# First attention layer of a two-layer diffusion trunk: both halves of a unit's value product in one attention step

## The chip, the cores and the metric

The kernel runs on one core of one Trainium2 chip. Times are device microseconds (us) of a whole execution. An execution's profile gives its span from the first to the last instruction; what lies around the span is the rest of the execution's time.

## The reference

The network has two layers over 1024 latent tokens and 256 context tokens, 1024 channels, 16 heads of 64. The first layer is windowed attention with grouped keys (4 key heads, each shared by 4 query heads), a sink logit for each head, rotary positions and a SiLU gate:

```python
q, k, v, g = _split_a(u @ w_in)
...
mask = (jnp.abs(qi[:, None] - kj[None, :]) <= A_WINDOW) & (kj >= 0)[None, :] & (kj < S)[None, :]
s_lat = jnp.einsum('bqkgd,bjkd->bkgqj', qb, kb).astype(jnp.float32) * scale
...
p = jax.nn.softmax(jnp.concatenate([s_lat, s_ctx, s_sink], axis=-1), axis=-1)
...
o = jnp.einsum('bkgqj,bjkd->bqkgd', p_lat, vb) + jnp.einsum('bkgqc,bckd->bqkgd', p_ctx, vc)
...
y = (o * jax.nn.silu(g)) @ w_out
```

A block of 128 queries sees the 128-key blocks before, at and after it, and the 256 context keys. Context queries see the context alone. The second layer (neighbourhood attention) is not touched by the change.

## The kernel before, in words

Every fp32 operand of a matmul is held as a high part and a rest (`hi`, `lo`), and a product is made of two or three matmuls. So a 512-column piece of a projection takes three matmuls at each of eight depths (L208, L209, L210).

**Sub-blocks and units.** The first layer's attention is cut into 160 sub-blocks (`subsA`, L686), ordered by head pair p (8), query block b (10; blocks 8 and 9 are the context), head h (2). Sub-block k = 20p + 2b + h. The two heads of one (p, b) are a unit, and its value product is made for both heads at once. For one sub-block the engines do:

- TensorE (PE): the scores S, four matmuls into a PSUM tile `psbig` (L704, L705; two matmuls for context queries).
- VectorE (DVE): scale, mask and row minimum, L317, called M here. It reads S out of PSUM.
- ScalarE (ACT): the exponential with its sum, L324. GpSimd (POOL) writes the sink column ahead of it (L322).
- DVE: the reciprocal, L328; POOL: the product with it, L329 (both in `sm_second`).
- PE: up to five 128x128 transposes T into another `psbig` tile (L336). ACT copies the high part out, `pth` (L340); DVE makes the rest, `ptl` (L342).
- PE, once for a unit: the value product (L733), at most five matmuls of 256 columns with `pth` (part 0) and as many with `ptl` (part 1). For every second block the result leaves PSUM through ACT (L742), DVE (L743) and POOL (L746), which multiplies it into the gate.

There are two `psbig` buffers, shared by S and T (L98), three buffers for the softmax rows `s` (L309) and two each for `pth` and `ptl` (L344).

**Steps.** `att_steps` (L752) lists the attention as steps. Step k holds `sm_second` of sub-block k+1 and T of k (`t_piece`), then S of sub-block k+3 (`s_piece`), then value work. With `split=True` part 0 of a unit stands in the step two after its last sub-block and part 1 in the step after that, so each step holds five value matmuls. Each piece has a cost (545 for T, 545 for S, 1090 for a whole unit's value product).

**Fill.** `merge` (L284) lays projections between the pieces: the gate projection of head pair p and the query projection of pair p+1 (48 pieces), in proportion to the cost of the attention pieces that have been laid down. The last pair has the output projection of the first token block as fill, and its last six attention pieces come after the two gate transposes (L843 to L848). In pairs 0 to 6, modulation work (`dots`: DVE L617, POOL L618, ACT L599, with a DMA of 256 KB each) and loads of the next keys and values are put into the list of pieces at fixed positions.

**Order.** The list is recorded in this order; the framework's scheduler then sets each engine's order, with attention's M, exponential and rest lifted ahead (`lift`), and places tiles in the buffers. Each engine runs its own list in order.

Of the kernel before, what the change touches and what calls it, by code (L numbers as in the profile page):

```python
# [34 lines left out]
AHEAD_A, LIFT_A = 3, 80  # L35
# [47 lines left out]
def build(tc, i, out):  # L83
# [16 lines left out]
    def psone(name):  # L100
        return ps.tile([P, 512], F32, tag="one", bufs=4, name=name)
# [26 lines left out]
    def lift(n):  # L128

        return tc.high_priority(n) if n else nullcontext()  # L130
# [196 lines left out]
    def sm_second(s):  # L327
        nc.vector.reciprocal(s.rs, s.sum)  # L328
        nc.gpsimd.tensor_scalar(s.t[:, : s.w], s.t[:, : s.w], s.rs, 1.0, ALU.mult, ALU.mult)  # L329
# [356 lines left out]
    subsA = [(p, b, h) for p in range(8) for b in range(10) for h in range(2)]  # L686
    stA, ptA, pvA = {}, {}, {}

    def tilesA(b):
        if b >= 8:  # L690
            return [8, 9]
        return list(range(max(0, b - 1), min(8, b + 2))) + [8, 9]
# [32 lines left out]
    def pvA_fn(p, b, part):  # L725
        if b % 2 == 0 and part == 0:
            pvA[p] = psone(f"pvA{p}_{b}")
        o = pvA[p][:, (b % 2) * 256 : (b % 2) * 256 + 256]
        tl = tilesA(b)
        pt = ptA[p, b]  # L730
        for k, t in enumerate(tl):
            x = (pt.lo if part else pt.hi)[:, k].rearrange("p h q -> p (h q)")
            mm(o, vA[p // 2][:, t, :], x, start=k == 0 and not part, stop=part == 1 and k == len(tl) - 1)  # L733
        if not part:
            return
        del ptA[p, b]
        if b % 2 == 1:
            tmp = px.tile([P, 2, P], F32, tag="otmp", bufs=1, name="otmp")
            pv = pvA[p].rearrange("p (b h q) -> p b h q", b=2, h=2)
            for h in range(2):  # L740
                hs = slice(h * 64, h * 64 + 64)
                nc.scalar.copy(tmp[hs], pv[64:128, :, h, :])  # L742
                nc.vector.tensor_tensor(tmp[hs], pv[0:64, :, h, :], tmp[hs], ALU.add)  # L743
            tok = slice((b - 1) * P, (b + 1) * P)
            g = gA[p][:, tok]
            nc.gpsimd.tensor_tensor(g, tmp.rearrange("p b q -> p (b q)"), g, ALU.mult)  # L746
            if p == 7:
                dma(ogd[0][p][:, tok], g)
            elif b == 9:
                dma(ogd[0][p], gA[p])  # L750

    def att_steps(subs, qk, st, tr, pv, last_of_unit, costs, need, ahead, rise, split=False):  # L752

        seq = []
        n = len(subs)
        for k in range(-ahead, n + 2 + split):
            row = []

            def t_piece(k=k):
                if k + 1 < n:  # L760
                    with lift(rise(k)):
                        sm_second(st[k + 1])
                if k >= 0:
                    tr(k)

            def s_piece(k=k):
                qk(k + ahead)

            def v_piece(k=k):
                pv(k - 2)  # L770

            def v_first(k=k):
                pv(k - 2, 0)

            def v_second(k=k):
                pv(k - 3, 1)

            if -1 <= k < n:
                row.append((costs[0] if k >= 0 else 0.0, t_piece, 0))
            if k + ahead < n:  # L780
                row.append((costs[1], s_piece, 0))
            if split and 0 <= k - 2 < n and last_of_unit(k - 2):
                row.append((costs[2] / 2, v_first, 0))
            elif split and k - 3 >= 0 and last_of_unit(k - 3):
                row.append((costs[2] / 2, v_second, need(k - 3, k + ahead)))
            elif not split and k - 2 >= 0 and last_of_unit(k - 2):
                row.append((costs[2], v_piece, need(k - 2, k + ahead)))
            seq.append(row)
        return seq
# [3 lines left out]
    def needA(k, kq):  # L793
# [4 lines left out]
        c = (b >= 4) + (b >= 8)  # L798
        return G7_AT[c] if p == 7 else 8 * (c + 1)

    rowsA = att_steps(
        subsA, qkA, stA, trA, lambda k, x: pvA_fn(*subsA[k][:2], x), lambda k: subsA[k][2] == 1,
        (545, 545, 1090), needA, AHEAD_A, lambda k: LIFT_A, True,
    )
    k_load(0, 0)
    k_load(0, 1)
# [400 lines left out]
    for b in range(8):  # L1207
        x = ob.tile([P, D], F32, tag="x", bufs=2, name="x")
# [130 lines left out]
```

## Time and profile before

| | us |
|---|---|
| median of three runs | 1449.84 (1449.49 to 1455.52) |
| the profiled execution | 1450.25 |
| its span | 1448.5 |
| busy in the span: PE, DVE, ACT, POOL | 1393.6, 988.8, 733.9, 631.7 |
| steps of the first layer's attention | from 105 to 588 in the span |

The first layer's attention, with its projections as fill, is a third of the span. After it come the first layer's output and normalisation (to about 700), the second layer's attention (to about 1320) and its output.

In a timeline row the first number is the start in us from the span's start, the second the duration, then engine, line, operation, `out<-in`, shape and count. A bracket says how long the engine stood idle before and what ended that. In rows grouped by line, the two numbers behind the first bar are the group's busy time in us and the mean duration of one instruction in ns. PEld is the weight load of PE. PE's matmuls are pipelined: one starts before the one ahead of it has ended.

### The profile page before, as it was taken

How to read it: one execution, taken by the hardware profiler on the slowest of the kernel's cores; microseconds unless marked ns; L12 is line 12 of the kernel's file. 1: busy time of each engine (PE TensorE's matmuls, PEld its weight loads, DVE VectorE, ACT ScalarE, POOL GpSimd, SP SyncE). 2: the span in 40 equal slices, each digit the busy share in tenths (PEclk: the TensorE clock that was granted, in tenths of full speed). 3: DMA queues.
4: the chain of work that ended last, by engine and by line, in shares of the span. 5: the costliest groups of instructions: out<-in, count | busy, mean ns of one | idle time of the engine just before them, and what ended most of it. 6: DMA issues, size and time to landing. Idle time of an engine off the chain costs nothing. (4 is left out here: it accounts for less than half of the span.)

```text
span 1448.5 us, 25148 instructions
## 1 busy us (share of the span) xinstructions
PE 1393.6 (96%) x8815; PEld 1217.2 (84%) x8816; DVE 988.8 (68%) x2216; ACT 733.9 (51%) x1561; POOL 631.7 (44%) x779
## 2 busy tenths in 40 slices
PE   8998999999999999999999999999999999998995
PEld 5887888888888888788888899888988898887775
DVE  4658887878888789566423766555565565667698
ACT  4336776677676778332222545554454444557310
POOL 0326666666666657233301333333233333336664
PEclk9999999999999999999999999999999999999998
DMA  9472114123222124434278565565555564384353
GB/s 369 172 227 85 60 48 131 45 77 101 68 70 62 56 67 131 133 129 136 75 216 230 156 195 152 150 166 146 168 147 152 146 182 140 102 207 151 114 133 93
DMA packets 117229, 195.05 MB, mean 135 GB/s; under 512 B 9328, under 2 KB 57840, under 8 KB 117104
## 3 DMA queue, kind: packets, MB, share of 16 engines
q1 hardware_dynamic: 117104, 193.45, 44.4%
q8 instruction: 70, 1.15, 0.3%
q14 instruction: 55, 0.45, 0.1%
HBM read 141.51 MB, written 51.90 MB: 134 GB/s over the span
## 5 line engine op out<-in xcount | busy, mean ns | idle before, releaser
L329 POOL TENSOR_SCALAR s_B<-s_B,rs_B 128x640 f32<-128x640 f32 (+1 forms) x128 | 101.1, 790 | 298.0 <-DVE rs_B L328 243.9
L208 PE MATMUL pj<-uBh,wh 128*128 128x512 f32 (+1 forms) x448 | 176.0, 393 | 0.0
L209 PE MATMUL pj<-uBl,wh 128*128 128x512 f32 (+1 forms) x448 | 170.3, 380 | 0.0
L210 PE MATMUL pj<-uBh,wl 128*128 128x512 f32 (+1 forms) x448 | 170.1, 380 | 0.0
L324 ACT ACTIVATE s_B<-s_B,m_B 128x640 f32<-128x640 f32 (+1 forms) x128 | 102.9, 804 | 131.2 <-DVE m_B L317 131.1
L324 ACT ACTIVATE s_A<-s_A,m_A 128x641 f32<-128x641 f32 (+2 forms) x160 | 119.5, 747 | 88.7 <-DVE m_A L317 73.7
L164 POOL TENSOR_TENSOR wl<-wr,wh 128x512 fp32r<-128x512 f32 x64 | 87.7, 1370 | 162.1 <-ACT wh L162 139.8
L329 POOL TENSOR_SCALAR s_A<-s_A,rs_A 128x640 f32<-128x640 f32 (+2 forms) x160 | 126.8, 793 | 58.0 <-DVE rs_A L328 55.7
L317 DVE CUSTOM_DVE_ANT_0 s_A<-S_A,msk,nsk 128x640 f32<-128x640 f32 (+2 forms) x160 | 123.6, 774 | 34.1 <-PE S_A L705 17.7
L342 DVE TENSOR_TENSOR pt_B<-T_B,pt_B 128x640 fp32r<-128x640 f32 (+1 forms) x128 | 100.9, 788 | 61.0 <-ACT pt_B L340 60.6
L208 PE MATMUL pj<-uAh,wh 128*128 128x512 f32 (+1 forms) x384 | 140.0, 365 | 0.0
L209 PE MATMUL pj<-uAl,wh 128*128 128x512 f32 (+1 forms) x384 | 137.8, 359 | 0.0
L210 PE MATMUL pj<-uAh,wl 128*128 128x512 f32 (+1 forms) x384 | 137.5, 358 | 0.0
L342 DVE TENSOR_TENSOR ptl_A<-T_A,pth_A 128x640 fp32r<-128x640 f32 (+2 forms) x160 | 114.0, 713 | 15.3 <-PE pvA L733 7.1
L336 PE MATMUL T_A<-ident,s_A 128*128 128x128 f32 x672 | 101.1, 275 | 12.2 <-DVE m_A L317 8.9
L336 PEld LDWEIGHTS T_A<-ident,s_A 128*128 128x128 f32 x672 | 77.2, 140 | 40.2 <-issue 16.7
L340 ACT CAST pt_B<-T_B 128x640 fp32r<-128x640 f32 (+1 forms) x128 | 84.3, 658 | 47.6 <-PE T_B L336 46.6
L317 DVE CUSTOM_DVE_ANT_0 s_B<-S_B,bias 128x640 f32<-128x640 f32 (+1 forms) x128 | 100.4, 784 | 10.5 <-PE S_B L1036 9.7
L340 ACT CAST pth_A<-T_A 128x640 fp32r<-128x640 f32 (+2 forms) x160 | 96.4, 603 | 16.8 <-PE T_A L336 14.1
L210 PEld LDWEIGHTS pj<-uBh,wl 128*128 128x128 f32 x448 | 84.3, 188 | 16.6
L336 PE MATMUL T_B<-ident,s_B 128*128 128x128 f32 x608 | 88.7, 275 | 9.9 <-DVE pt_B L342 5.0
L242 PE MATMUL pv<-wh,uBh 128*128 128x256 f32 x320 | 92.8, 291 | 3.1 <-ACT wh L162 3.1
(219 smaller groups left out, 3883.6 us busy)
## 6 DMA issues: line engine op xcount, KB each, us to landing
kB<-kdB SPq DMA_DIRECT2D x64, 320.0 KB, 5.2
gw<-in_wadaT SPq DMA_DIRECT2D x48, 256.0 KB, 2.8
vdB<-st SPq DMA_DIRECT2D x20, 512.0 KB, 3.2
vB<-vdB SPq DMA_DIRECT2D x16, 640.0 KB, 4.7
wada<-in_wadaC SPq DMA_DIRECT2D x16, 512.0 KB, 9.6
kdB<-st SPq DMA_DIRECT2D x16, 512.0 KB, 3.0
qdB<-st SPq DMA_DIRECT2D x16, 512.0 KB, 3.5
qB<-qdB SPq DMA_DIRECT2D x32, 256.0 KB, 4.7
```

The lines of the kernel that those rows point to most:

```text
L164: e.tensor_tensor(lo, r, f32(hi), ALU.subtract)
L208: mm(pt[:, :n], hi[:, sl], rh, start=kt == 0, stop=False)
L209: mm(pt[:, :n], hi[:, sl], rl, start=False, stop=False)
L210: mm(pt[:, :n], lo[:, sl], rh, start=False, stop=kt == KT - 1)
L242: mm(pt, lh, hi[:, sl], start=kt == 0, stop=False)
L317: nc.vector.tensor_tensor_reduce(outp, sc, in1, scale, init if init is not None else 3e38, ALU.add, ALU.min, accum_out=s.m)
L324: nc.scalar.activation(s.t[:, :n], s.t[:, :n], AF.Exp, bias=s.m, scale=-1.0, accum_out=s.sum)
L329: nc.gpsimd.tensor_scalar(s.t[:, : s.w], s.t[:, : s.w], s.rs, 1.0, ALU.mult, ALU.mult)
L336: nc.tensor.transpose(tp[:, k * P : (k + 1) * P], s.t[:, src * P : (src + 1) * P], ident)
L340: nc.scalar.copy(pt.hi[:, :n, hl, :], tv)
L342: nc.vector.tensor_tensor(pt.lo[:, :n, hl, :], tv, f32(pt.hi[:, :n, hl, :]), ALU.subtract)
```

## The change

`att_steps` gets no `split`, and a new function makes both parts of a unit's value product in one piece of cost 1090, two steps after the unit's last sub-block:

```diff
+    def pvA_both(k):
+        for part in range(2):
+            pvA_fn(*subsA[k][:2], part)
+
     rowsA = att_steps(
-        subsA, qkA, stA, trA, lambda k, x: pvA_fn(*subsA[k][:2], x), lambda k: subsA[k][2] == 1,
-        (545, 545, 1090), needA, AHEAD_A, lambda k: LIFT_A, True,
+        subsA, qkA, stA, trA, pvA_both, lambda k: subsA[k][2] == 1,
+        (545, 545, 1090), needA, AHEAD_A, lambda k: LIFT_A,
     )
```

Part 0 stays in its step; part 1 comes one step earlier. Every second step now holds a whole unit's value product, and the steps between hold none. `merge` gives a step fill in proportion to its cost, so the steps with values (2180) get twice the fill of those without (1090). Pair p's list has 50 pieces in place of 60, so the inserted `dots` and loads stand at other places in it, and the last six pieces of the last pair (`att[-6:]`) begin three steps earlier: T of sub-block 157, then the values of the units that end at 155, T of 158 and 159, and the values of the last two units.

PE's order before, in the middle of the third head pair (sub-blocks 48 and 51; `pj` are projection matmuls, `pvA` value matmuls); the next row is T of 49:

```order
L336 MATMUL T_A48_3134<-ident_63,s_A48_3006 128x128 x5
L704 MATMUL S_A51_3142<-kA1_0_2126,qA5_2427 128x384
L705 MATMUL S_A51_3142<-kA1_0_2126,qA5_2427 128x256
L704 MATMUL S_A51_3142<-kA1_1_2682,qA5_2427 128x384
L705 MATMUL S_A51_3142<-kA1_1_2682,qA5_2427 128x256
L208 MATMUL pj20_0_3092<-uAh0_105,wh20_2685 128x512
L209 MATMUL pj20_0_3092<-uAl0_108,wh20_2685 128x512
L210 MATMUL pj20_0_3092<-uAh0_105,wl20_2686 128x512
L733 MATMUL pvA2_2_3121<-ptl_A44_2953,vA1_2167 128x256 x5
L208 MATMUL pj20_0_3092<-uAh0_105,wh21_2689 128x512
L209 MATMUL pj20_0_3092<-uAl0_108,wh21_2689 128x512
L210 MATMUL pj20_0_3092<-uAh0_105,wl21_2690 128x512
```

The same step after; here T of 49 is the last row:

```order
L336 MATMUL T_A48_3139<-ident_63,s_A48_3006 128x128 x5
L208 MATMUL pj20_0_3092<-uAh0_105,wh20_2685 128x512
L209 MATMUL pj20_0_3092<-uAl0_108,wh20_2685 128x512
L210 MATMUL pj20_0_3092<-uAh0_105,wl20_2686 128x512
L704 MATMUL S_A51_3150<-kA1_0_2172,qA5_2426 128x384
L705 MATMUL S_A51_3150<-kA1_0_2172,qA5_2426 128x256
L704 MATMUL S_A51_3150<-kA1_1_2682,qA5_2426 128x384
L705 MATMUL S_A51_3150<-kA1_1_2682,qA5_2426 128x256
L208 MATMUL pj20_0_3092<-uAh0_105,wh21_2689 128x512
L209 MATMUL pj20_0_3092<-uAl0_108,wh21_2689 128x512
L210 MATMUL pj20_0_3092<-uAh0_105,wl21_2690 128x512
L336 MATMUL T_A49_3167<-ident_63,s_A49_3067 128x128 x5
```

The step keeps its six projection matmuls and loses its five value matmuls; three of the projections now stand ahead of S, so three in place of six and five value matmuls lie between S and the next T. The step after it (T of 49) has ten value matmuls.

DVE's order before, where the third pair's second half begins (`ra`, `rb` and `qA`, L472 and L660, bring the next pair's queries out; `otmp` is L743):

```order
L342 TENSOR_TENSOR ptl_A50_3207<-T_A51_3260,pth_A50_3206 128x5x128
L472 TENSOR_TENSOR ra_3231<-ra_3231,rb_3232 128x512
L328 RECIPROCAL rs_A54_3282<-sum_A54_3281 128x1
L743 TENSOR_TENSOR otmp_3248<-pvA2_2_3121,otmp_3248 64x256
L660 TENSOR_TENSOR qA6_3237<-ra_3231,qA6_3237 64x512
L317 ISA s_A55_3315,m_A55_3316<-S_A55_3310,msk_141,nsk_142 128x512
L317 ISA m_A55_3316 128x1
L660 TENSOR_TENSOR qA7_3238<-ra_3231,qA7_3238 64x512
L342 TENSOR_TENSOR ptl_A52_3301<-T_A52_3302,pth_A52_3300 128x5x128
```

The same place after:

```order
L342 TENSOR_TENSOR ptl_A50_3218<-T_A51_3260,pth_A50_3217 128x5x128
L472 TENSOR_TENSOR ra_3230<-ra_3230,rb_3231 128x512
L328 RECIPROCAL rs_A54_3276<-sum_A54_3275 128x1
L660 TENSOR_TENSOR qA6_3236<-ra_3230,qA6_3236 64x512
L660 TENSOR_TENSOR qA7_3237<-ra_3230,qA7_3237 64x512
L317 ISA s_A55_3323,m_A55_3324<-S_A55_3318,msk_141,nsk_142 128x512
L317 ISA m_A55_3324 128x1
L342 TENSOR_TENSOR ptl_A52_3306<-T_A52_3307,pth_A52_3305 128x5x128
```

Both L660 now stand ahead of M of 55, and `ptl` of 52 follows M with nothing between.

## The prediction

> **What bounds the kernel now.** I read the page first, then busy time by stretches, then the waits and the timeline of the first layer's attention, where all of the change lies.
>
> ```profile
> PE 1393.6 (96%) x8815; PEld 1217.2 (84%) x8816; DVE 988.8 (68%) x2216; ACT 733.9 (51%) x1561; POOL 631.7 (44%) x779
> ```
>
> PE is busy for 96% of the span, so the question is what the change does to PE's idle time.
>
> ```profile
> core 0: us, PE busy (x) PEld busy (x) DVE busy (x) ACT busy (x) POOL busy (x), PEclk, DMA share, GB/s
> 110.00:170.00 60.00, 54.56 (x360) 47.79 (x359) 50.17 (x124) 42.19 (x97) 41.06 (x57) 1.00 0.23 68
> 170.00:230.00 60.00, 58.77 (x384) 51.11 (x382) 48.40 (x120) 41.68 (x97) 40.21 (x57) 1.00 0.27 82
> 410.00:470.00 60.00, 58.81 (x386) 51.66 (x385) 48.76 (x120) 41.06 (x93) 39.04 (x57) 1.00 0.22 67
> ```
>
> In the attention PE is idle 1.2 of 60 us in a good stretch and 5.4 at the start, at a granted clock of 1.00. DVE is next, busy 48.4 of 60: it has some 20% to spare in the mean, not in every step. What PE and DVE wait for from 110 to 592:
>
> ```profile
> PE T_A L336 <- DVE m_A L317: 8.9, 16, 1.6
> PE S_A L704 <- DVE ptl_A L342: 5.1, 7, 1.2
> PE S_A L705 <- DVE ptl_A L342: 1.8, 6, 0.3
> PE T_A L336 <- POOL gw L618: 1.3, 1, 1.3
> ```
>
> ```profile
> DVE ptl_A L342 <- PE pvA L733: 7.1, 14, 1.2
> ```
>
> PE's waits are for the two `psbig` buffers: T or S waits until DVE has read what stands in one, by M (L317) or by `ptl` (L342). They come to 17.1 us in all. That is what the change could save by these rows; it takes no work from PE. DVE itself waits 7.1 us until value matmuls have read a `ptl` tile.
>
> By the Trainium skill's Perfetto Trace Analysis, Identifying the Most-Contended Engine, matmul busy time is a poor measure of the room that is left, and the weight loads' busy share a better one. By it the room from 170 to 230 would be 60 - 51.11 = 8.9 us in place of 1.2, and a gain not bounded by 17.1. The trace agrees that PE's busy time hides some waits: below, S at 313.83 starts as `ptl` ends (312.96 + 0.82 = 313.78), 0.64 after T where 0.47 is usual, and its row shows no idle time.
>
> Now a step without a wait, from 319.61, and one with:
>
> ```profile
> 312.16 0.88 DVE L317 CUSTOM_DVE_ANT_0 s_A<-S_A,msk,nsk 128x640 f32<-128x640 f32 x1
> 312.96 0.82 DVE L342 TENSOR_TENSOR ptl_A<-T_A,pth_A 128x640 fp32r<-128x640 f32 x1
> 313.19 0.73 PE L336 MATMUL T_A<-ident,s_A 128*128 128x128 f32 x5 [0.24 <-DVE m_A L317]
> 313.83 0.44 PE L704 MATMUL S_A<-kA,qA 128*128 128x384 f32 x1
> ...
> 319.61 0.71 PE L336 MATMUL T_A<-ident,s_A 128*128 128x128 f32 x5
> 320.08 0.42 PE L704 MATMUL S_A<-kA,qA 128*128 128x384 f32 x1
> 320.41 0.70 ACT L340 CAST pth_A<-T_A 128x640 fp32r<-128x640 f32 x1 [0.53 <-PE T_A L336]
> 320.62 0.28 PE L705 MATMUL S_A<-kA,qA 128*128 128x256 f32 x1
> 320.74 0.39 PE L208 MATMUL pj<-uAh,wh 128*128 128x512 f32 x1
> 320.97 0.40 PE L209 MATMUL pj<-uAl,wh 128*128 128x512 f32 x1
> 321.05 0.88 DVE L317 CUSTOM_DVE_ANT_0 s_A<-S_A,msk,nsk 128x640 f32<-128x640 f32 x1 [0.97 <-POOL s_A L329]
> 321.44 0.75 PE L733 MATMUL pvA<-ptl_A,vA 128*128 128x256 f32 x5
> 322.03 0.39 PE L208 MATMUL pj<-uAh,wh 128*128 128x512 f32 x1
> 322.72 0.71 PE L336 MATMUL T_A<-ident,s_A 128*128 128x128 f32 x5
> ```
>
> From start to start the prices are: T 0.47, S 0.66, a 512-column matmul 0.23, five value matmuls 0.59. The step is 0.47 + 0.66 + 6 x 0.23 + 0.59 = 3.10; measured 3.11.
>
> **The change, part by part.**
>
> *Work.* All instructions stay; PE's sum is the same. 0.
>
> *Light and heavy steps.* Two steps of 3.10 become a light one, 0.47 + 0.66 + 1.38 = 2.51, and a heavy one, 3.69. DVE's M, `ptl` and reciprocal stay one a step. Does the light step leave room for the chain from one buffer use to the next?
>
> Floor 1, T in the buffer of the S just made. S's last matmul ends at 320.62 + 0.28 = 320.90, M starts 0.15 later and takes 0.88, and T may start 0.15 after M (312.16 + 0.88 = 313.04 against 313.19). So T comes 1.34 after PE is free of S (320.74) at the earliest. Before, 1.97 of PE work lies there; in the light step 0.69. It would be 0.65 late.
>
> Floor 2, T in the buffer of the T before it:
>
> ```profile
> 128.74 0.73 PE L336 MATMUL T_A<-ident,s_A 128*128 128x128 f32 x5 [0.55 <-DVE m_A L317]
> ...
> 130.24 0.83 DVE L342 TENSOR_TENSOR ptl_A<-T_A,pth_A 128x640 fp32r<-128x640 f32 x1 [0.23 <-ACT pth_A L340]
> 131.21 0.74 PE L336 MATMUL T_A<-ident,s_A 128*128 128x128 f32 x5
> ```
>
> From T to T through `pth` and `ptl` is 2.47, under the light step's 2.51. In the built program before, T nearly always takes S's buffer; after, 55 steps have under 1.07 of PE work behind S (10 before), and in 47 of the 55 T takes T's buffer. So the likely answer is that light steps just fit. Going through all steps of both orders with these prices and the floor of each (M and `ptl` shorter for narrow blocks), the work falls short of the floor in 30 steps before, by 4.0 us together, and in 29 after, by 6.0. I take the difference, **+2.0**. From below: 0, where other waits cover it. From above: in a light step S then follows M, which follows `ptl` (2.33 + 0.88 + 0.15 = 3.36 after T, where PE is at 2.51 + 0.47 + 0.23 = 3.21): 0.15 in each of 45 more light steps is 6.7.
>
> *DVE's order.* A projection's evacuation on DVE makes the same waits in each pair:
>
> ```profile
> 266.31 0.75 DVE L317 CUSTOM_DVE_ANT_0 s_A<-S_A,msk,nsk 128x512 f32<-128x512 f32 x1
> ...
> 267.10 0.69 DVE L660 TENSOR_TENSOR qA<-ra,qA 64x512 fp32r<-64x512 f32 x1
> 267.44 0.71 PE L336 MATMUL T_A<-ident,s_A 128*128 128x128 f32 x5
> ...
> 268.69 0.51 PE L705 MATMUL S_A<-kA,qA 128*128 128x256 f32 x2 [0.31 <-DVE ptl_A L342]
> ...
> 279.25 0.41 PE L336 MATMUL T_A<-ident,s_A 128*128 128x128 f32 x2 [0.16 <-DVE m_A L317]
> 280.34 0.39 PE L704 MATMUL S_A<-kA,qA 128*128 128x256 f32 x1 [0.67 <-DVE ptl_A L342]
> ```
>
> That is 0.31 + 0.16 + 0.67 = 1.14 a pair. After, both L660 stand ahead of M, so `ptl` is early and the 0.31 goes; but M ends 0.69 later, and T, which had 267.44 - 267.06 - 0.15 = 0.23 to spare, waits 0.46. The 0.67 goes too, since `ptl` of 56 comes ahead of the L660. In its place M of 61 stands behind a `dot` and `ptl` of 58, in the queue of a light step; I estimate that at one L617:
>
> ```profile
> L617 DVE CUSTOM_DVE_ANT_0 gj<-gw,gh 128x512 f32<-128x512 f32 x48 | 38.1, 794 | 1.4 <-DMA gw<-in_wadaT 1.0
> ```
>
> 0.79 less the 0.15 gap is 0.64, so the pair pays 0.46 + 0.64 = 1.10. Net **0**. Bounds: all seven pairs save their 1.14 (-8.0), or all pay 1.10 more (+7.7). The moved `dots` and key loads on SP's queue pass at most each other and the weight loads of the next projection, which are two pieces ahead; 0, at worst one late `dot`, as in the 1.3 wait on `gw` above, in each pair.
>
> *The values' own waits.* Part 1 a step earlier gives `ptl` its buffer back a step earlier, so most of DVE's 7.1 goes. Part 1 itself now comes two steps, about 6 us, after the T it needs, and `ptl` ends 2.33 after T (131.07 against 128.74), so no new wait arises there. PE's waits on `ptl` above stand behind L660, not behind these: I take **0**, at most -7.1.
>
> *The tail.* Both gate transposes now stand ahead of the last three T, and each needs an ACT copy:
>
> ```profile
> 584.34 1.01 ACT L368 COPY gates<-gate 128x1024 f32<-128x1024 f32 x1 [0.49 <-PE gate L367]
> 587.49 0.50 PE L419 MATMUL yA<-woAh,og 128*128 128x512 f32 x1 [0.88 <-ACT gates L368]
> ```
>
> Before, one copy costs PE 0.88. After, T of 157 waits for the first copy, T of 158 for the second, T of 159 for `ptl` of 157, with few matmuls between: two thirds of each copy and 0.2 for the rest is 1.5. **+0.6** (0 to +2).
>
> The sum is 2.0 + 0 + 0 + 0.6 = +2.6 on the profiled execution's 1450.25, so 1452.9. That execution lies 0.4 above the median of the three, so I forecast **1452.5**, which is no change by a bound of 0.5% (7.25 us, about what a measurement of this kernel can tell from none).
>
> **The rivals.**
>
> *Slower: light steps are too short for DVE.* In a light step M and `ptl` must both be made while PE does 2.51 us, and anything that stands ahead of them in DVE's queue (a `dot`, a reciprocal that waits for ACT, L660) goes straight to PE. For it: floor 1 misses by 0.65, floor 2 fits by 0.04 only. Against it: the two steps together leave DVE as much time as before. If a third of the 45 extra light steps lose 0.65 and the others 0.15, it is 9.8 + 4.5 = 14.3, with the 2.6 above +16.9: **1467**. It decides from (7.25 - 2.6) / 45 = 0.10 us a light step.
>
> *Faster: buffers come back earlier.* `ptl` and its buffer a step earlier keep DVE's queue ahead. All of PE's S waits (5.1 + 1.8) and half of T's 8.9 go, 11.4, less the tail's 0.6: **1439**. Against it: DVE's 7.1 lie where PE was not waiting, as far as I looked.
>
> *The clock drops.* Its granted value has one dip near the second layer's start:
>
> ```profile
> 727.00:734.00 7.00, 5.17 (x32) 5.17 (x33) 1.90 (x7) 0.62 (x1) 0.00 (x0) 0.76 0.71 210
> ```
>
> ```profile
> 728.83 0.80 PE L242 MATMUL pv<-wh,uBh 128*128 128x256 f32 x2 [3.15 <-ACT wh L162]
> ```
>
> A wait of 3.15 us goes with 7 us at 0.76, which costs 7 x 0.24 = 1.7 us. If light steps cause one dip in each of the 8 pairs, it is 13.6 + 2.6: 1466. Against it: waits up to 1.6 us in the attention left the clock at 1.00. TensorE: Matmul & The Clock Gate in the Trainium skill, A second HAM failure mode: psum-queue depth-cycling, describes this: frequent short idles between matmul groups that cycle through PSUM make the gate swing. The trace so far does not bear it out in this attention.
>
> That the change does nothing is no rival: the order of PE differs in nearly every step.
>
> **How the numbers follow.** No change, as summed: 0.58. Light steps too short: 0.28. Clock: 0.02. Buffers earlier: 0.12. So faster by over 0.5% is 0.12, within it 0.58, slower 0.30. The range is 1442 to 1469: the lower end is the sum with the 7.1 and half of the pairs' 1.14 gone (1452.5 - 7.1 - 3.4); the upper holds the slower rival at 1467 with the tail's upper bound. That leaves out most of the faster rival and the slower one's upper part, about 0.2 in all.
>
> **What would show it.** Right: PE's waits from 110 to 592 stay within 15 to 22 us; T waits more on `ptl` and less on M; DVE's wait on `pvA` is nearly gone; the waits at sub-blocks 56 and 60 are replaced by one before T of 53. Wrong: light steps of over 2.7 us throughout (slower), PE's waits under 10 us (faster), or a granted clock under 1.00 between 110 and 590.

## The result, and the profile after

The kernel after takes **1459.23 us** (median of four runs, 1456.89 to 1464.67) against 1449.66 for the kernel before on the same chip (four runs, 1447.81 to 1455.52). The ratio is 1.0076 with a 95% interval of 1.0057 to 1.0095: slower by 0.6 to 1.0%, some 8 to 14 us. The forecast was 1452.5 with 1442 to 1469. The time lies within the range, but not in the case taken for the likeliest (no change); it stands between that and the rival "light steps are too short for DVE" (1467). The range held because that rival set its upper bound; the sum behind the forecast, +2.6 us, is far from the measured +9.6.

The profiled execution took 1461.1 us with a span of 1459.3 (before 1450.25 and 1448.5). The page's first line, as before, gives the busy time of each engine:

```profile
PE 1396.3 (96%) x8816; PEld 1216.8 (83%) x8816; DVE 985.7 (68%) x2216; ACT 733.3 (50%) x1561; POOL 633.3 (43%) x779
```

The work is the same to some 3 us on every engine. PE's span grew by 10.8 us and its busy time by 2.7, so what was lost is time in which PE waited. The same three stretches as in the prediction, busy time of PE, PEld, DVE, ACT and POOL, then the granted clock:

```profile
110.00:170.00 60.00, 55.25 (x361) 47.84 (x361) 51.31 (x123) 41.27 (x95) 42.74 (x57) 1.00 0.22 69
170.00:230.00 60.00, 57.94 (x379) 50.44 (x378) 47.62 (x118) 41.61 (x96) 38.83 (x56) 1.00 0.29 82
410.00:470.00 60.00, 58.23 (x382) 51.17 (x381) 48.80 (x124) 41.91 (x96) 41.02 (x59) 1.00 0.18 58
```

The start of the attention is a little better (54.56 before), the good stretches are worse by 0.6 to 0.8 (58.77 and 58.81 before), and the clock stayed at 1.00 in this execution. What PE waits for from 110 to 600, in us, times, longest:

```profile
PE T_A L336 <- DVE m_A L317: 10.3, 18, 1.3
PE T_A L336 <- DVE ptl_A L342: 3.9, 11, 0.9
PE T_A L336 <- POOL s_A L329: 3.7, 5, 1.0
PE S_A L704 <- DVE ptl_A L342: 3.7, 3, 1.2
PE pvA L733 <- ACT pth_A L340: 2.2, 3, 1.6
```

T now waits for `ptl`, as forecast, but no less for M. ACT's `pth` (2.2) is new as a releaser, and POOL's scaling of the softmax (L329) has grown to 3.7 from this row of the kernel before:

```profile
PE T_A L336 <- POOL s_A L329: 0.2, 1, 0.2
```

DVE's own waits in the same stretch, after:

```profile
DVE ptl_A L342 <- ACT pth_A L340: 25.5, 50, 2.1
DVE otmp L743 <- ACT otmp L742: 12.3, 30, 1.3
DVE qA L660 <- ACT qA L659: 6.3, 10, 0.7
DVE gj L617 <- DMA gw<-in_wadaT: 7.0, 5, 2.3
```

The 7.1 us for `pvA` have gone, as forecast. In their place DVE waits for ACT (the first two rows were 5.1 and 4.5 before), and 7.0 us for loads of the dots (1.0 before).

Where PE's time went shows when the third pair of heads is cut in two: its inner blocks (five tiles wide), and its edge, the narrow blocks 8 and 9 with the next pair's block 0, where the next pair's queries are also made. First the kernel before:

```profile
242.00:267.00 25.00, 23.84 (x161) 21.36 (x160) 19.11 (x43) 16.65 (x37) 15.15 (x21) 1.00 0.16 53
268.00:293.00 25.00, 23.83 (x153) 20.45 (x152) 22.35 (x59) 16.87 (x45) 18.77 (x28) 1.00 0.14 43
```

and the kernel after, the second row 26 us long:

```profile
243.00:268.00 25.00, 24.66 (x165) 22.00 (x164) 18.80 (x45) 17.82 (x39) 16.38 (x23) 1.00 0.16 51
269.00:295.00 26.00, 23.31 (x153) 20.24 (x154) 21.62 (x54) 17.17 (x43) 17.18 (x25) 1.00 0.13 42
```

Inside, PE's idle time falls from 1.16 to 0.34 us. At the edge it rises from 1.17 to 2.69. The third figure of the rows behind the length is DVE: before, it is busy for 19.11 of 25 us inside, 76%, and for 22.35 of 25 at the edge, 89%. The prediction read 48.4 of 60 over a stretch that holds both, 81%.

All 156 steps from T3 to T158 can be booked in this way: the time from one T to the next, less the step's matmuls at the spacing seen in the timeline (0.232 us for 512 columns, 0.175 for 384, 0.118 for 256, 0.093 for a transposition of 128). "Inner" are the steps 4 to 13 of the pairs 0 to 6, "edges" the other steps before T143. What is left over, in us:

| | before | after | difference |
|---|---|---|---|
| inner, light steps (even) | 8.4 | 14.4 | +6.0 |
| inner, heavy steps (odd) | 13.2 | 7.8 | -5.4 |
| edges | 19.9 | 25.1 | +5.2 |
| last pair, from T143 | 6.2 | 9.8 | +3.6 |
| sum | 47.7 | 57.1 | +9.4 |

Inside, the light steps wait and the heavy ones win it back. The account is coarse: in a run told below, an edit of the last pair's end alone leaves 27.6 us at the edges in place of 25.1. Two waits at the edge of the third pair, in the timeline of the kernel after (POOL, DVE, ACT and PE):

```profile
278.70 1.29 POOL L164 TENSOR_TENSOR wl<-wr,wh 128x512 fp32r<-128x512 f32 x1
...
279.07 1.47 DVE L660 TENSOR_TENSOR qA<-ra,qA 64x512 fp32r<-64x512 f32 x1 [0.69 <-ACT qA L659]
...
280.57 0.48 DVE L317 CUSTOM_DVE_ANT_0 s_A<-S_A,msk,nsk 128x256 f32<-128x256 f32 x1
...
281.20 0.41 PE L336 MATMUL T_A<-ident,s_A 128*128 128x128 f32 x2 [1.22 <-DVE m_A L317]
...
285.16 1.31 POOL L618 TENSOR_TENSOR gw<-gw,gh 128x512 f32<-128x512 f32 x1 [2.22 <-DVE rs_A L328]
...
286.44 1.01 POOL L329 TENSOR_SCALAR s_A<-s_A,rs_A 128x256 f32<-128x256 f32 x1
...
287.50 0.44 PE L336 MATMUL T_A<-ident,s_A 128*128 128x128 f32 x2 [0.95 <-POOL s_A L329]
```

Before T of 57, M of 59, which frees the buffer that T takes, stands behind an L660, which waited 0.69 for ACT and took 1.47 in place of its usual 0.69. Before T of 59, POOL's half of a dot (L618, 1.31) stands ahead of the scaling that T needs. Neither place was in the prediction; T of 53, which was, waits 0.33 where 0.46 was forecast; the 0.64 forecast behind M of 61 did not come.

The last pair loses at a place that was not looked at either, a cast of the output weights (L359) on ACT:

```profile
566.39 0.62 ACT L359 CAST woAh<-wor 128x512 fp32r<-128x512 f32 x1 [1.43 <-DMA wor<-in_wAo]
...
568.26 0.69 ACT L340 CAST pth_A<-T_A 128x640 fp32r<-128x640 f32 x1
...
569.00 0.85 PE L733 MATMUL pvA<-pth_A,vA 128*128 128x256 f32 x5 [1.63 <-ACT pth_A L340]
...
573.38 0.74 PE L336 MATMUL T_A<-ident,s_A 128*128 128x128 f32 x5 [1.31 <-DVE m_A L317]
```

The cast waits 1.43 us for its load, `pth` stands behind it on ACT, and value matmuls wait 1.63 for `pth`.

### The profile page after: what moved, and what is told of

It reads as the page before. It is cut to its first block, busy times and chain, and to the rows that moved or that the text cites. A ratio compares the mean times of both kernels' runs of the same rounds, so it can differ in the third digit from the quotient of the medians.

```text
span 1459.3 us, 25100 instructions
## 1 busy us (share of the span) xinstructions
PE 1396.3 (96%) x8816; PEld 1216.8 (83%) x8816; DVE 985.7 (68%) x2216; ACT 733.3 (50%) x1561; POOL 633.3 (43%) x779
## 5 line engine op out<-in xcount | busy, mean ns | idle before, releaser
L329 POOL TENSOR_SCALAR s_B<-s_B,rs_B 128x640 f32<-128x640 f32 (+1 forms) x128 | 101.7, 795 | 296.1 <-DVE rs_B L328 252.8
L329 POOL TENSOR_SCALAR s_A<-s_A,rs_A 128x640 f32<-128x640 f32 (+2 forms) x160 | 125.7, 789 | 84.1 <-DVE rs_A L328 75.0
L164 POOL TENSOR_TENSOR wl<-wr,wh 128x512 fp32r<-128x512 f32 x64 | 87.0, 1360 | 159.9 <-ACT wh L162 133.1
L208 PE MATMUL pj<-uAh,wh 128*128 128x512 f32 (+1 forms) x384 | 143.7, 374 | 0.0
L336 PE MATMUL T_A<-ident,s_A 128*128 128x128 f32 x672 | 101.9, 276 | 21.8 <-DVE m_A L317 10.3
```

The lines of the kernel that those rows point to most:

```text
L164: e.tensor_tensor(lo, r, f32(hi), ALU.subtract)
L208: mm(pt[:, :n], hi[:, sl], rh, start=kt == 0, stop=False)
L336: nc.tensor.transpose(tp[:, k * P : (k + 1) * P], s.t[:, src * P : (src + 1) * P], ident)
```

## The experiments

Each ratio is against the kernel before on the same chip, with its 95% interval; after is 1.0076 (1.0057 to 1.0095). The theories, as the expectations name them: **L**, light steps leave DVE and ACT too little time, plainly because steps are unequal, or more narrowly because no value matmuls lie between S and the next T; **D**, dots and L660 stand badly in DVE's queue; **E**, the end of the last pair; **V**, part 1 and the values' evacuation come too early; **R**, only the edges and the last pair cost; **G**, the dots' loads come late.

**The steps evened.** Each piece's share of the projection is its cost: a light step (even k, the first triple) now gets most of it. Dots and the order of the pieces stay.

```diff
-        (545, 545, 1090), needA, AHEAD_A, lambda k: LIFT_A,
+        ((985, 985, 0), (263, 263, 263)), needA, AHEAD_A, lambda k: LIFT_A,
```

> The kernel after, with the projection's matmuls shared out so that both kinds of step hold about the same matmul work (in the built order 2.87 us of work in a step without values and 2.70 in one with both parts, against 2.48 and 3.10 after). Values, evacuations, dots and the end of the last pair stay as in after. Theory L (light steps leave DVE and ACT too little time between S and T): most of what the attention lost before the last pair's end comes back, 1450 to 1454. Theory D (the dots and L660 stand badly in DVE's queue in the pairs 43 to 63 and 83 to 103, whatever the steps' weight): 1457 to 1460. Theory E (the loss is at the end of the last pair alone): 1457 to 1460.

Measured: 1453.64 us, **1.0036** (1.0023 to 1.0050). About half of the loss is back and half is not. In the account of the steps the inner ones now leave 14.4 us, less than before the change (21.6), and the edges 29.6, more than after. So evening helps inside and does not mend the edges. Of the 29.6, 3.4 us are two falls of the clock, of which the last section shows one.

**Before, made uneven.** The opposite: one part of the values a step as in before, but the projection shared out so that steps alternate.

```diff
-        (545, 545, 1090), needA, AHEAD_A, lambda k: LIFT_A, True,
+        ((200, 200, 400), (890, 890, 1780)), needA, AHEAD_A, lambda k: LIFT_A, True,
```

> The kernel before (one part of the values a step), with the projection's matmuls shared out unevenly, so that steps alternate between 2.31 and 3.26 us of matmul work as they do after (2.48 and 3.10); the value matmuls still lie behind S in every step. Theory L in its plain form (unequal steps alone cost): 1455 to 1460. Theory L in its narrower form (what costs is that no value matmuls lie between S and the next T in a light step): 1448 to 1452. Theories D and E: 1448 to 1452.

Measured: 1448.73 us, **1.0001** (0.9990 to 1.0011). Unequal steps alone cost nothing that can be measured. L in its plain form falls.

**The dots put back.** The change shortened the list of pieces, into which dots and loads are inserted by count, so it had moved them by up to a step. Here they stand between the steps where before has them (`old` is the list with as many pieces as in before).

```diff
-                att.insert(3 + g * (n // SEG[p] + 1), dots.pop(0))
+                old.insert(3 + g * (n // SEG[p] + 1), [dots.pop(0)])
+            att = [x for piece in old for x in piece]
```

> The kernel after, with the dots and the loads of keys and values put back between the same steps as before. Theory D: the about 2 us that each of the pairs 43 to 63 and 83 to 103 lost come back, 1454 to 1456. Theories L and E: 1458 to 1461.

Measured: 1458.13 us, **1.0067** (1.0054 to 1.0081). Not told apart from after. The edges of the third and fifth pair went back to what they left before (2.4 us each; 2.6 before, 4.5 and 4.2 after), but as much was lost elsewhere, 2.52 us of it in one place, shown in the last section. D explains these two edges and not the loss.

**The last pair's end.** The last transpositions stand among the projection's matmuls again.

```diff
-            merge(att[:-6], fill, lead=1500.0)
+            merge(att[:-3], fill, lead=1500.0)
-            merge(att[-6:], [])
+            merge(att[-3:], [])
```

> The kernel after, with three pieces in place of six left over behind the gate transposes at the end of the last pair, so that the last transposes T157 and T158 stand among the projection's matmuls again, as before. Theory E (the end of the last pair cost 4 to 5 us, where the prediction had 0.6): 1453 to 1456. Theory L and the prediction's +0.6 for the tail: 1458 to 1461.

Measured: 1456.53 us, **1.0060** (1.0046 to 1.0073). At most a small part; the intervals overlap. The last pair leaves 7.2 us in this run's account, where it left 9.8 after and 6.2 before.

**Both parts a step later.** Part 0 moved back in place of part 1 forward (`v_late` calls `pv(k - 3)`).

```diff
-            elif not split and k - 2 >= 0 and last_of_unit(k - 2):
-                row.append((costs[2], v_piece, need(k - 2, k + ahead)))
+            elif not split and k - 3 >= 0 and last_of_unit(k - 3) and late:
+                row.append((costs[2], v_late, need(k - 3, k + ahead)))
```

> The kernel after, with both parts of the values one step later (three steps behind the unit's last transposes in place of two), so that part 0 is moved back in place of part 1 forward. Steps stay unequal (2.21 and 3.37 us of matmul work). Theory L (a light step without value matmuls behind S): no better than after, 1457 to 1464. Theory V (part 1 and the evacuation of the values come a step too early and stand ahead of pth and ptl in ACT's and DVE's queues): 1448 to 1453.

Measured: 1466.47 us, **1.0131** (1.0118 to 1.0144), worse than after. V finds no support. The run does not test it cleanly, though, since the later values bring a wait that the kernel after does not have, ACT's `pth` behind the value matmuls:

```profile
ACT pth_A L340 <- PE pvA L733: 43.3, 47, 2.3
```

**A light step's projection behind S.** There are 1.39 us of work from S to the next T in a light step, in place of 0.70; both parts of the values stay in the heavy step.

```diff
-        (545, 545, 1090), needA, AHEAD_A, lambda k: LIFT_A,
+        ((0, 1090, 0), (545, 545, 1090)), needA, AHEAD_A, lambda k: LIFT_A,
```

> The kernel after, with all of a light step's projection matmuls behind its S: from S to the next T there is 1.39 us of work in place of 0.70, while steps stay as unequal as after (2.27 and 3.31 us). Theory L in the narrower form (what costs is too little work between S and the next T): 1451 to 1456, as much as evening the steps brought, or more. Theory L in the plain form (unequal steps): 1458 to 1462.

Measured: 1458.50 us, **1.0073** (1.0058 to 1.0088). No better than after. The narrower form of L fails here too, at least as a remedy by other matmuls: what is put behind S is taken from between T and S. Its trace has falls of the clock in the attention, 10.2 us at half the granted clock (from 160.30 and from 221.74), which cost some 5 us. Without them its account would be 53.6 us against 57.1 after, so the waits are somewhat fewer and the time is not.

**Three edits together:** steps evened, dots put back, last pair's end restored (the diffs above).

> The kernel after, with the steps evened, the dots put back between the steps of before, and the last pair's end as in before: the three edits together. By the three runs alone (1.0036, 1.0067 and 1.0060 against 1.0076 for after) they bring 5.8 + 1.3 + 2.3 us: 1449 to 1451 if the losses are separate, that is nothing left of the slowdown. If they are the same loss seen in three ways, 1453 to 1454, no better than evening alone.

Measured: 1451.19 us, **1.0019** (1.0009 to 1.0029). Most of the loss is back and a small rest is left: nearer to "separate losses" than to "one loss seen in three ways". The rest, 2.6 us by the mean of the executions, is as large as what this run loses more to the clock (last section).

**Before, with the values ahead of S.** One part a step and equal steps, but the value matmuls no longer lie between S and the next T.

```diff
-            if k + ahead < n:
-                row.append((costs[1], s_piece, 0))
             if split and 0 <= k - 2 < n and last_of_unit(k - 2):
...
+            if k + ahead < n:
+                row.append((costs[1], s_piece, 0))
             seq.append(row)
```

> The kernel before (one part of the values a step, equal steps), with the value matmuls ahead of S in place of behind it: from S to the next T there is 0.70 us of work in nearly every step in place of 1.98. Theory L in the narrower form: slower than before, 1453 to 1461. Theory L in the plain form (unequal steps) and theory V: 1447 to 1451.

Measured: 1457.73 us, **1.0071** (1.0059 to 1.0083). With not one step made unequal, this costs as much as the whole change. So having the value matmuls ahead of S has a price. Where it is paid is less plain. The same two stretches of the third pair of this run, inside and edge:

```profile
245.00:270.00 25.00, 24.16 (x161) 21.44 (x160) 18.43 (x44) 17.27 (x38) 15.64 (x22) 1.00 0.17 53
271.00:296.00 25.00, 23.48 (x152) 20.17 (x151) 23.12 (x58) 16.89 (x45) 17.77 (x26) 1.00 0.17 54
```

Inside, PE is busy for 24.16 us of 25, more than in the kernel before (23.84), with DVE at 74%. At the edge it is 23.48 (23.83 before) with DVE at 92%. The two nearly cancel in this pair. Over all pairs the account of the steps has them cancel in part: 24.9 us at the edges (19.9 before), 18.4 inside (21.6 before), 7.7 in the last pair (6.2 before), so only 3.4 us more from T of 3 on. More is lost ahead of T of 3, in the start of the attention, here first before and then this run:

```profile
0.00:113.70 113.70, 109.54 (x851) 89.00 (x852) 65.02 (x130) 45.62 (x94) 24.30 (x28) 1.00 0.72 253
0.00:113.12 113.12, 105.91 (x824) 85.96 (x824) 64.37 (x128) 45.75 (x93) 23.23 (x27) 0.98 0.72 254
```

PE starts 27 matmuls fewer there in nearly the same time, idles for 7.2 us in place of 4.2, and the clock falls once, which costs another 1.7. So this run alone does not place the price at the edges. It and the next three turn the question from what kind of step into where the step is.

**Both parts in one step, inner blocks only** (1 to 5 of the pairs 0 to 6), the rest as in before:

```diff
+    def bothA(k):
+        p, b, _ = subsA[k]
+        return p < 7 and 1 <= b <= 5
...
+            if split and 0 <= k - 2 < n and last_of_unit(k - 2) and both(k - 2):
+                row.append((costs[2], v_both, need(k - 2, k + ahead)))
```

> The kernel before, with both parts of the values in one step only for the inner blocks 1 to 5 of the heads' pairs 0 to 6, so that the light and heavy steps lie only where all blocks are five tiles wide; blocks 6 to 9 and 0, the last pair, and the dots stay as in before. Theory R (the inner light steps wait but the heavy ones win it back; the loss lies at the pairs' edges and in the last pair): 1447 to 1451. Theory L (light steps cost wherever they are): half or more of the loss, 1453 to 1457.

Measured: 1446.29 us, **0.9993** (0.9980 to 1.0006). No cost.

**Both parts in one step, edges only:** the same with `p < 7 and not 1 <= b <= 5`.

> The complement: both parts in one step only for blocks 6 to 9 and 0 of the pairs 0 to 6; the inner blocks, the last pair and the dots stay as in before. Theory R: 1452 to 1456. Theory L: 1451 to 1453, about half of the loss at most.

Measured: 1459.57 us, **1.0079** (1.0066 to 1.0092): the whole loss, more than R itself expected. The two complements add up to what the change does (-0.0007 + 0.0079 = 0.0072 against 0.0076), with 0.6 us left for the last pair, uncertain by some 4 us, so that the account's +3.6 there is neither shown nor shut out. The same two stretches of the run with inner blocks only:

```profile
240.00:265.00 25.00, 24.87 (x169) 22.19 (x168) 18.92 (x45) 17.08 (x38) 15.70 (x23) 1.00 0.22 71
266.00:291.00 25.00, 24.43 (x160) 21.00 (x159) 22.67 (x61) 18.15 (x45) 18.92 (x27) 1.00 0.14 43
```

PE's idle time inside is 0.13 us of 25 (1.16 in before) and at the edge 0.57 (1.17 in before). In the run with edges only, most of the added wait falls not on the edge steps themselves (22.2 us, 19.9 before) but on the inner steps behind them (27.4, 21.6 before). This is one place, T of 48, first the kernel before:

```profile
251.70 0.74 PE L336 MATMUL T_A<-ident,s_A 128*128 128x128 f32 x5 [1.16 <-DVE m_A L317]
```

and then the run:

```profile
251.78 1.30 POOL L164 TENSOR_TENSOR wl<-wr,wh 128x512 fp32r<-128x512 f32 x1
252.12 1.51 DVE L617 CUSTOM_DVE_ANT_0 gj<-gw,gh 128x512 f32<-128x512 f32 x1 [1.00 <-DMA gw<-in_wadaT]
...
253.56 0.88 DVE L317 CUSTOM_DVE_ANT_0 s_A<-S_A,msk,nsk 128x640 f32<-128x640 f32 x1
...
254.59 0.74 PE L336 MATMUL T_A<-ident,s_A 128*128 128x128 f32 x5 [1.73 <-DVE m_A L317]
```

DVE waits 1.00 for a dot's load, the dot takes 1.51 in place of 0.68, M stands behind it, and T waits 1.73. Then the granted clock falls to 0.50 for 3.4 us, which costs as much again (1.7 us):

```profile
252.39:255.80 3.41, 1.68 (x10) 1.12 (x10) 3.35 (x7) 1.24 (x3) 2.24 (x4) 1.00 0.24 77
255.80:259.22 3.42, 3.42 (x13) 2.93 (x13) 1.48 (x4) 1.80 (x5) 1.42 (x2) 0.50 0.02 5
```

**Inner blocks, evened:** the inner run with costs of 1167 for T and S of a light step and 312 for each piece of a heavy one.

> The inner blocks as in the run with both parts there, but with the projection's matmuls shared out evenly over the two kinds of step (2.93 and 3.14 us of work); the rest as in before. By the idle time of the evened run (14.4 us in the inner steps against 21.6 before and 22.2 after) it should be faster than before if the edges are left as they were: 1441 to 1446. If evening only moves the waits to the edges, as that run's edges (29.6 us against 19.9 before) suggest: 1447 to 1451.

Measured: 1447.51 us, **0.9997** (0.9988 to 1.0005). No gain: in its account the inner steps leave 15.5 us (21.6 before) and the edges 25.8 (19.9 before). Evening only moves the waits, and no version here beats the kernel before.

**The dots without their loads.** Each dot multiplies the resident `gh` tiles, so the adaptive-norm sums leave out their weights; all instructions on DVE, POOL and ACT stay.

```diff
-            dma(t, i["wadaT"][j, :, h * 512 : (h + 1) * 512])
-            nc.vector.tensor_tensor_reduce(o, t, gh[0], 0.5, 0.0, ALU.mult, ALU.add, accum_out=acc[:, j, 0:1])
-            nc.gpsimd.tensor_tensor(t, t, gh[1], ALU.mult)
+            nc.vector.tensor_tensor_reduce(o, gh[1], gh[0], 0.5, 0.0, ALU.mult, ALU.add, accum_out=acc[:, j, 0:1])
+            nc.gpsimd.tensor_tensor(t, gh[0], gh[1], ALU.mult)
```

> The kernel after with the loads of the dots' weights left out: each dot multiplies the resident gh tiles in place of a loaded gw tile, so the adaptive-norm sums are not the reference's. DVE, POOL and ACT keep all their instructions. Theory G (the dots' loads come late and hold DVE's queue, 7.0 us of waits in after against 1.0 in before, with M and ptl behind them): most of the loss goes, 1448 to 1453. If the late loads only fill time that DVE had, and the order of M, ptl and L660 at the pairs' edges costs by itself: 1456 to 1460.

Measured: 1461.35 us, **1.0096** (1.0079 to 1.0113). The 7.0 us of waits for loads are gone from DVE's rows, and nothing is won. G falls: PE's waits on M rose from 10.3 to 12.8. (L703 is L704 of the other kernels.)

```profile
PE T_A L336 <- DVE m_A L317: 12.8, 18, 1.3
PE S_A L703 <- DVE ptl_A L342: 4.7, 3, 1.6
```

## Why the prediction was right or wrong

**Work, 0:** right; PE's and DVE's busy time moved by 3 us each in opposite directions.

**Light and heavy steps, +2.0 (0 to 6.7):** right in its sum for the inner blocks, from which its rows came, and less so step by step. Light steps do wait, 6.0 us more in all, and the heavy ones return 5.4. The run with inner blocks only bounds their cost at -2.9 to +0.9 us, so the +2.0 was somewhat too much. The term was then carried to all 55 light steps. The rival's price of 0.10 us a light step, above which it decides, was passed by the inner light steps (6.0 over 35 is 0.17), but what the heavy steps return leaves 0.02. The rival had no such return in its sum. What costs in the third pair are a few single waits, the longest 1.22 and 0.95 us.

**DVE's order, net 0 (-8.0 to +7.7):** the step that failed, as far as the runs show it. It says what a pair pays at its edge, 1.14 us before and 1.10 after. By the run with edges only the change there costs 9.6 to 13.3 us, above the upper bound, of which some 2.5 us go with the clock (last section). The edges have light steps too, and no run separates these there from DVE's order; but the waits can be named. For the third pair, the three that the prediction named as going (0.31, 0.16, 0.67) were replaced by 0.33, 0.31, 1.22 and 0.95, of which only the first was foreseen. Two things were left out of the sum. L660 was priced at 0.69 and took 1.47 ahead of M of 59. And POOL, whose own queue holds L618 and L164 of 1.3 us each, was taken as free: T's waits for L329, one of 0.2 us in before, came to 3.7.

**The values' own waits, 0 (to -7.1):** right as a price. DVE's 7.1 went, and no gain of PE's shows for it. The value matmuls wait for `pth` three times, 2.2 us; these are of part 0, which the term did not look at.

**Dots' loads, 0, at worst one late dot a pair:** five were late, 7.0 us of DVE's time, more than the forecast and within its worst case; yet the run without the loads shows that the price for PE was indeed about nothing.

**The tail, +0.6 (0 to +2):** the runs leave about 0.6 us for it (0.0076 less 0.0072 of 1448), with an uncertainty of some 4 us. Its mechanism was wrong: in the trace no gate copy is late, but a load of the output weights.

**The lower bound** takes 3.4 us for half of the seven pairs' 1.14, which is 4.0; nothing hangs on it.

**The rivals.** The clock stayed at 1.00 from 110 to 590 in the profiled execution, so the clock is out for what this trace shows. In some of the other runs it did fall there (last section). Buffers earlier: out, since T's waits on M did not fall. Light steps too short: the right sign and nearest in size, with the right engine, but placed in every step. **What would show it:** PE's waits left the band of 15 to 22 us (the five rows above alone are 23.8), which marked the forecast case as wrong, a true mark. The rival's mark, light steps of over 2.7 us throughout, could not tell: 27 of the 35 light steps inside took longer than that, and so did 29 of the same 35 in the kernel before, since the projection is not shared out so evenly that a light step holds 2.51 us of work (by the account's spacing it is 2.66 in the mean inside, and 2.90 before).

**Shown:** the loss comes with the values of the edge blocks and not with those of the inner blocks, and it needs neither the dots' shift nor their loads. **Argued only:** that this is because DVE is 89% busy at the edge and 76% inside, so that a late M is not made good before the next. No run gave DVE less to do at the edge alone, and in the run with edges only most of the added wait stands in the inner steps behind. **Open:** which of L660, the evacuations and the dots sets the price at each edge. That evening gave no more than half of the loss back is in part the clock's doing: the run is 4.8 us above the kernel before by the mean of the executions, and 3.2 of it go with the clock.

## What to carry to other kernels

Read the spare time of the engine that feeds the bottleneck by stretches no longer than one phase of the work: 81% busy over a pair was 76% inside, where the change was free, and 89% at the edge, whose blocks brought all of the loss. Before taking matmuls out of a gap, ask in which phases that gap may be the cover for someone else's queue, and try the change by phases. And when a step of the sum is a list of waits with offsetting signs, its bounds are only as good as the list: price every engine in the chain, the idle-looking ones too, at the longest duration that its rows show there.

## What the runs showed of the hardware

**DVE and POOL hold each other up.** The rows of L660 and L617 of the kernel after (count, then min, median and max in ns):

```profile
L660 DVE TENSOR_TENSOR qA<-ra,qA x32: 684/690/1674, 93.3 to 530.2; 64x512 fp32r<-64x512 f32 x32
...
L617 DVE CUSTOM_DVE_ANT_0 gj<-gw,gh x48: 670/682/1503, 114.5 to 521.6; 128x512 f32<-128x512 f32 x48
```

One of the long dots in the timeline:

```profile
346.05 1.29 POOL L164 TENSOR_TENSOR wl<-wr,wh 128x512 fp32r<-128x512 f32 x1
...
346.38 1.50 DVE L617 CUSTOM_DVE_ANT_0 gj<-gw,gh 128x512 f32<-128x512 f32 x1
```

The same instruction takes 0.69 or up to 1.67, and 0.68 or 1.50. In the long cases quoted here (L660 at 279.07 and L617 at 346.38, and L617 at 252.12 in the run with edges only) a POOL instruction had started 0.33 to 0.37 us earlier, and DVE's ended 0.54 to 0.55 behind its end. The Trainium skill, SBUF — State Buffer, SBUF: two separate sides, describes this: VectorE and GpSimd share a pair of ports under an exclusive lock, held for the whole instruction, and a VectorE instruction with two SBUF inputs takes part in it. These two have two SBUF inputs, and the trace agrees. L660's other form, which reads `pj` from PSUM, took its usual 0.42 at 285.29 while POOL's L618 ran. The other way round, POOL's L329 took 1.01 at 286.44, while an L617 ran, where the same shape took 0.48 at 277.04. So the order of POOL against DVE is a term of the sum; the two lines of the rows above were busy for 61.3 us before and 62.2 after from 110 to 600, so the stretches were hardly longer in total, but they fell ahead of other instructions.

**A wait of under 2 us can halve the clock, or not, by where it falls.** In the evened run T of 78 waits 1.91 us, and then 512-column matmuls start 0.43 apart in place of 0.23:

```profile
346.26 0.41 PE L336 MATMUL T_A<-ident,s_A 128*128 128x128 f32 x2 [1.91 <-DVE ptl_A L342]
...
347.21 0.63 PE L208 MATMUL pj<-uAh,wh 128*128 128x512 f32 x1
347.64 0.63 PE L209 MATMUL pj<-uAl,wh 128*128 128x512 f32 x1
```

In the run with the dots put back T waits longer, 2.52 us, and the clock stays at 1.00:

```profile
313.10 0.73 PE L336 MATMUL T_A<-ident,s_A 128*128 128x128 f32 x5 [2.52 <-DVE m_A L317]
```

So the length of the wait alone does not decide it. The traces show what does. In the evened run the granted clock falls to 0.50 at 12.66, 347.17, 470.05 and 1337.03 us, and these times lie 98, 36 and 254 times 3.413 us apart. In the same way every trace here with two or more falls has them a whole number of 3.413 us apart, and up to the last 30 us each lasts for that time, twice or three times it. Cut at such borders, the evened run and then the run with the dots put back show (length, busy time of the engines with PE first, clock):

```profile
343.76:347.17 3.41, 1.50 (x8) 0.99 (x7) 3.10 (x9) 1.75 (x6) 2.48 (x3) 1.00 0.47 101
347.17:350.59 3.42, 3.42 (x12) 2.90 (x11) 0.88 (x3) 1.08 (x3) 1.80 (x3) 0.50 0.59 176
```

```profile
308.47:311.88 3.41, 2.11 (x13) 1.54 (x11) 2.32 (x4) 3.06 (x7) 3.12 (x4) 1.00 0.51 154
311.88:315.30 3.42, 2.20 (x17) 2.23 (x18) 3.20 (x9) 1.91 (x4) 3.07 (x4) 1.00 0.28 77
```

The wait of 1.91 us lies within one stretch, in which PE is busy for 1.50 us; the next stretch runs at half the clock, which costs 3.41 x 0.5 = 1.7 us on top of the wait. The wait of 2.52 us lies across a border, PE is busy for over 2 us on either side, and the clock stays. Over all fourteen traces, up to their last 30 us, each of the 23 stretches with 1.81 us or more of PE's idle time was followed by a fall, one of six with 1.73 to 1.80 was, and none with less while the clock was at 1.00. This rule is read from these traces; no run was made to test it.

The clock is thus a part of the price of waits, and of the differences between runs. As an estimate, the time that an execution loses to it is its span times what its mean granted clock lacks of 1. In the mean of the executions this is 7.4 to 8.2 us in the kernel before where it was timed beside the runs, 10.2 after and with edges only, 10.8 with the three edits, 11.3 evened and 11.7 with the values ahead of S. So some 2 us of what the change costs go with the clock, and the rest is waits.
